# Nine of sixteen contraction steps with seven products, and one sum of weight blocks made by an accumulating DMA

## The chip, the cores and the metric

The kernel runs on one core of a Trainium2 chip. The metric is device time in microseconds (us) of one execution; a profiled execution gives the trace that the views below are taken from. TensorE (PE) does the matrix products, VectorE (DVE) and ScalarE (ACT) the elementwise work, GpSimd (POOL) and SyncE (SP) mostly issue DMAs.

## The reference

The input x has 256 rows (tokens) of 4096 float32 values. Only the attention layer is run (DEPTH is 1), then a final norm:

```python
h = x
h = h + attn_branch(rms_norm(h, norm_attn), w_in_attn, w_out_attn)
return rms_norm(h, final_norm)

def attn_branch(xn, w_in, w_out):
    proj = xn @ w_in                       # 256 x 4096 by 4096 x 16384
    q, k, v, g = jnp.split(proj, 4, axis=-1)
    ...                                    # 32 heads of 128, strictly causal stick-breaking attention
    return (o * jax.nn.silu(g)) @ w_out    # 256 x 4096 by 4096 x 4096
```

Almost all of the work is in the two projections. Their weights are 335 MB, which are read once.

## The kernel before

**Products.** Every float32 operand is split into a high part (cast to fp32r, `wh`, on ScalarE, line 176) and the residual (`wl`, VectorE, function `minus`, line 102). One block product is three matmuls (`mm3`, lines 406 to 408): high by high, low by high, high by low. A block product is a 128x128 block of the rows' side (stationary) by a 128x512 block of weights (moving), summed in one of seven PSUM banks.

**Units and steps.** The projection with w_in is 16 units; each takes a set of 1024 columns, as two groups of 512. The projection with w_out is three units of 1024 columns and two single ones of 512. A unit walks the contraction in 16 steps of 256. A step has a 2x2 of row blocks (two halves of the tokens, two chunks of 128 of the contraction) and a 2x2 of weight blocks (two chunks, two column groups): B11, B21, B12, B22. The plain way takes eight block products. By Strassen and Winograd's scheme seven are enough, but then sums of blocks are needed on both sides. Units 0 and 1 and the first w_out unit are "plain"; 14 w_in units and 2 w_out units are "mixed": the steps in `SEVEN` (2, 4, 6, 8, 10, 12, 13) take seven products and the other nine take eight, in a form that shares the seven banks.

**Weights.** `load(q)` (line 155, SyncE's queue) brings a step's four blocks into one tile `raw` of 128 x 4 x 512 with four DMAs of 256 KB; three such tiles are in turn. `split(n)` makes `wh` and `wl` of one part of a step. A part is a pair of blocks (1024 columns wide) or a single one. In a seven-product step the blocks are used up as they are, B11 and B21's pair first, then B22 alone; then VectorE makes the sums in `raw` itself, a broadcast add of 1024 columns (L165) and two adds of 512 (L168, L169), and the sums are split as two more pairs. Tiles for split pairs are five (`PAIRS`), for singles one (`SINGLES`).

**Order.** The program walks the parts; before a part's products it emits `split` for the parts ahead until more than `PAIRS` pairs or `SINGLES` singles are in the window. Work beside the products (attention of the unit before, reading out the banks, loads) is put at a step of a unit by `at(u, s, ...)` and emitted after that step's products: transposes of the heads at steps 2 and 7, scores one step later, weights of the values and outputs at steps 5, 6, 10 and 11, `heads_parts` at 11 with three spills to DRAM on GpSimd's queue, `combine_early` at 14, `combine_late` at 15 (L352 to L355), the gate and the split of v (L375 to L386) at step 0 of the next unit. A scheduler then reorders instructions within each engine's queue. In the last w_in unit and behind it the spilled parts come back on GpSimd's queue (L485, L489).

**The end.** For the last `KEPT` (= `PAIRS`) parts the products of the second half of the tokens are kept until the first half has been read out, so that its norm and its stores lie beside them (`evac_out` with L537 and L538, `finish` with L554 to L570).

Of the kernel before, what the change touches and what calls it, by code (L numbers as in the profile page):

```python
# [9 lines left out]
F32 = mybir.dt.float32  # L10
# [3 lines left out]
ALU = mybir.AluOpType  # L14
# [4 lines left out]
P = 128  # L19
S = 256  # L20
# [4 lines left out]
CW = 256  # L25
# [15 lines left out]
SEVEN = (2, 4, 6, 8, 10, 12, 13)  # L41
SEVEN_OUT = SEVEN
RAW_BUFS = 3
PAIRS = 5
SINGLES = 1
# [7 lines left out]
EIGHT_FORMS = PLAIN_FORMS + ("S3", "S5")  # L53
SEVEN_FORMS = ("A11", "A12", "A22", "S2", "S3", "S4", "S1")
# [20 lines left out]
def kernel(  # L75
# [41 lines left out]
    for u, (kind, w, cols) in enumerate(units):  # L117
        for s in range(NS):
            if kind == "single":
                if s % 2 == 0:  # L120
                    quads.append(((w, cols[0], s), (w, cols[0], s + 1)))
                b = ((1, 6), (7, 2))[u - LAST + 1]
                which = [plain_part(slice(2 * (s % 2), 2 * (s % 2) + 2), *b)]
            else:
                quads.append(tuple((w, c, s) for c in cols))
                if kind == "plain":
                    which = [
                        plain_part(slice(0, 2), PLAIN["C11"], PLAIN["C21"]),
                        plain_part(slice(2, 4), PLAIN["C12"], PLAIN["C22"]),
                    ]  # L130
                else:
                    which = SEVEN_PARTS if s in (SEVEN if w is w_in else SEVEN_OUT) else EIGHT_PARTS
            for i, (place, prods) in enumerate(which):
                parts.append(
                    dict(u=u, s=s, i=i, last=i == len(which) - 1, place=place, prods=prods, quad=len(quads) - 1,
                         seven=which is SEVEN_PARTS, size=len(range(*place.indices(2 * KT))))
                )
# [7 lines left out]
    raw, wh, wl = {}, {}, {}  # L145

    def load(q):
        if q >= len(quads):
            return
        raw[q] = wp.tile([P, 2 * KT, W], F32, tag="raw", name=f"raw{q}", bufs=RAW_BUFS)  # L150
        for k, (w, blocks, s) in enumerate(quads[q]):
            for chunks in ([slice(0, 1), slice(1, 2)] if q == 0 else [slice(0, 2)]):
                to = slice(KT * k + chunks.start, KT * k + chunks.stop)
                for i, c in enumerate(blocks):
                    nc.sync.dma_start(raw[q][:, to, i * CW : (i + 1) * CW], w[c, s][:, chunks, :])  # L155

    def split(n):
# [4 lines left out]
        r = raw[q]  # L162
        if p["seven"] and p["i"] == 2:

            nc.vector.tensor_tensor(  # L165
                out=r[:, 0:3:2, :], in0=r[:, 0:4:3, :], in1=r[:, 2:3, :].broadcast_to([P, 2, W]), op=ALU.add
            )
            nc.vector.tensor_tensor(out=r[:, 3, :], in0=r[:, 0, :], in1=r[:, 3, :], op=ALU.add)  # L168
            nc.vector.tensor_tensor(out=r[:, 1, :], in0=r[:, 3, :], in1=r[:, 1, :], op=ALU.add)  # L169
# [4 lines left out]
        for c in ([slice(k, k + 1) for k in range(KT)] if n == 0 else [slice(0, size)]):  # L174
            f = r[:, place, :][:, c, :]
            nc.scalar.copy(wh[n][:, c, :], f)  # L176
            minus(wl[n][:, c, :], f, wh[n][:, c, :])
# [7 lines left out]
    def load_x(i):  # L185
        if i >= NS:
            return
        xs[i] = ap.tile([P, KT, S], F32, tag=("one", "two", "vh", "vl")[i % 4], name=f"xs{i}")
# [32 lines left out]
    def build(i, y, seven, what):  # L221
# [17 lines left out]
        tt(out=y[:, 3, :], in0=y[:, 1, :], in1=y[:, 3, :], op=ALU.subtract)  # L239
        tt(out=y[:, 1, :], in0=y[:, 0, :], in1=y[:, 1, :], op=ALU.subtract)  # L240
        tt(out=y[:, 0, :], in0=y[:, 3, :], in1=y[:, 0, :], op=ALU.subtract)
        tt(out=y[:, 2, :], in0=y[:, 2, :], in1=y[:, 0, :], op=ALU.add)
# [20 lines left out]
    load(0)  # L263
    load_x(1)
    load(1)
    load_x(2)
# [82 lines left out]
    def combine_late(bank, one, two):  # L349
# [3 lines left out]
        for t in (1, 0):  # L353
            tt(out=two[:, t, :], in0=bank[5], in1=two[:, t, :], op=ALU.subtract)
# [5 lines left out]
    def new_heads(u):  # L360

        st["qk", u] = ap.tile([P, NT, W], F32, tag="one", name=f"qk_sb{u}")
        st["gv", u] = ap.tile([P, NT, W], F32, tag="two", name=f"gv_sb{u}")
# [140 lines left out]
    def new_h(c):  # L504

        for t in range(NT):
            pool, tag = {NJ - 2: (wp, "s" + "hl"[t]), NJ - 1: (sp, "x" + "hl"[t] + "0")}.get(c, (ep, f"h{c}_{t}"))
            hs[c, t] = pool.tile([P, W], F32, tag=tag, name=f"h{c}_{t}")
# [142 lines left out]
    def products(n, rows=("A11", "A12", "A21", "A22", "S1", "S2", "S3", "S4", "S5")):  # L651
# [19 lines left out]
    for n, p in enumerate(parts):  # L671
# [10 lines left out]
        products(n, ("A11", "A12") if n >= n_parts - KEPT else PLAIN_FORMS + SEVEN_FORMS + ("S5",))  # L682
# [49 lines left out]
```

## Time and profile before

| | |
|---|---|
| median of three runs | 1792.67 us (1787.96 to 1793.42) |
| profiled execution | 1787.47 us, span 1785.8 us |
| mean granted TensorE clock | 0.996 |
| TensorE matmul, busy | 1765.1 us, 8059 instructions |
| VectorE, busy | 1539.7 us, 1885 instructions |
| ScalarE, busy | 1122.8 us, 1533 instructions |
| moved by DMA | 388.81 MB, mean 218 GB/s |

The span runs from the first to the last instruction; the profiled execution's own time is 1.7 us longer. In a view by line, a row has the line, the engine, the operation, out<-in with shapes and the count, then busy us and the mean ns of one, then the idle time before them and what ended it. In a timeline a row has the start, the duration, engine, line and operation, and in brackets the idle time before it. In a table of windows each engine has its busy us and instruction count in a stretch of the span, then the TensorE clock, the share of the DMA engines' time and GB/s.

### The profile page before, as it was taken

How to read it: one execution, taken by the hardware profiler on the slowest of the kernel's cores; microseconds unless marked ns; L12 is line 12 of the kernel's file. 1: busy time of each engine (PE TensorE's matmuls, PEld its weight loads, DVE VectorE, ACT ScalarE, POOL GpSimd, SP SyncE). 2: the span in 40 equal slices, each digit the busy share in tenths (PEclk: the TensorE clock that was granted, in tenths of full speed). 3: DMA queues.
4: the chain of work that ended last, by engine and by line, in shares of the span. 5: the costliest groups of instructions: out<-in, count | busy, mean ns of one | idle time of the engine just before them, and what ended most of it. 6: DMA issues, size and time to landing. Idle time of an engine off the chain costs nothing.

```text
span 1785.8 us, 23623 instructions
## 1 busy us (share of the span) xinstructions
PE 1765.1 (99%) x8059; PEld 1456.9 (82%) x8059; DVE 1539.7 (86%) x1885; ACT 1122.8 (63%) x1533; POOL 68.5 (4%) x135
## 2 busy tenths in 40 slices
PE   9999999999999999999999999999999999999997
PEld 7887888888888888888888888888888878888886
DVE  6678999989898989899999999989989888999863
ACT  6665666666666666666666666666666666665543
POOL 0001000000000000000000000000002201000000
PEclk9999999999999999999999999999999999999998
DMA  9966666566666666666666666757578978778874
GB/s 314 339 196 217 197 187 212 183 212 186 209 195 200 205 198 205 198 207 196 210 194 212 193 209 189 221 174 229 170 223 266 308 231 248 228 225 264 258 239 157
DMA packets 373993, 388.81 MB, mean 218 GB/s; under 512 B 23856, under 2 KB 351792, under 8 KB 373872
## 3 DMA queue, kind: packets, MB, share of 16 engines
q1 hardware_dynamic: 357296, 352.15, 62.7%
q0 software_dynamic: 14992, 32.78, 5.8%
q10 hardware_dynamic: 1584, 2.38, 0.4%
q8 instruction: 63, 1.03, 0.2%
q14 instruction: 58, 0.48, 0.1%
HBM read 370.43 MB, written 16.78 MB: 217 GB/s over the span
## 4 chain that ended last, share of the span: by engine, by line
PE 81%; issue 7%; DVE 4%; DMA 4%; ACT 3%; SPq 1%; POOL 0%; ACTq 0%; POOLq 0%; DVEq 0%
PE acc L406 26%; PE acc L407 26%; PE acc L408 25%; DVE wl L102 2%; ACT wh L176 2%; DMA xr<-in_x_dram 1%; DMA raw<-in_w_in_dram 1%; SPq L155 1%; PE tr L395 1%; DMA raw<-in_w_out_dram 1%; DMA xn<-in_xT_dram 0%; DVE raw L165 0%; DMA xres<-in_x_dram 0%; PE o L407 0%; PE o L408 0%
## 5 line engine op out<-in xcount | busy, mean ns | idle before, releaser
L102 DVE TENSOR_TENSOR wl<-raw,wh 128x1024 fp32r<-128x1024 f32 (+1 forms) x865 | 973.9, 1150 | 190.1 <-ACT wh L176 182.8
L176 ACT CAST wh<-raw 128x1024 fp32r<-128x1024 f32 (+1 forms) x865 | 833.5, 992 | 440.1 <-DVE raw L165 127.5
L406 PE MATMUL acc<-wh,nh 128*128 128x512 f32 x1694 | 669.0, 395 | 0.9 <-DVE qk_sb L352 0.6
L407 PE MATMUL acc<-wl,nh 128*128 128x512 f32 x1694 | 660.5, 390 | 0.0
L408 PE MATMUL acc<-wh,nl 128*128 128x512 f32 x1694 | 660.3, 390 | 0.0
L408 PEld LDWEIGHTS acc<-wh,nl 128*128 128x128 f32 x1694 | 318.0, 188 | 67.4
L407 PEld LDWEIGHTS acc<-wl,nh 128*128 128x128 f32 x1694 | 318.6, 188 | 63.7 <-DVE wl L102 2.8
L406 PEld LDWEIGHTS acc<-wh,nh 128*128 128x128 f32 x1694 | 318.1, 188 | 63.8 <-ACT wh L176 1.0
L165 DVE TENSOR_TENSOR raw<-raw 128x1024 f32<-128x1024 f32 x112 | 136.4, 1218 | 0.1
L407 PE MATMUL acc<-wl,ph 128*128 128x512 f32 x314 | 122.5, 390 | 0.4 <-DVE wl L102 0.2
L408 PE MATMUL acc<-wh,pl 128*128 128x512 f32 x314 | 122.2, 389 | 0.0
L406 PE MATMUL acc<-wh,ph 128*128 128x512 f32 x314 | 122.2, 389 | 0.0
L406 PE MATMUL acc<-wh,sh 128*128 128x512 f32 x256 | 100.3, 392 | 0.6 <-DVE sh L213 0.6
L408 PE MATMUL acc<-wh,sl 128*128 128x512 f32 x256 | 99.7, 390 | 0.6 <-DVE sl L216 0.6
L407 PE MATMUL acc<-wl,sh 128*128 128x512 f32 x256 | 99.9, 390 | 0.3 <-DVE wl L102 0.3
L168 DVE TENSOR_TENSOR raw<-raw 128x512 f32<-128x512 f32 x112 | 77.2, 689 | 2.7
L169 DVE TENSOR_TENSOR raw<-raw 128x512 f32<-128x512 f32 x112 | 76.9, 687 | 1.8
L407 PEld LDWEIGHTS acc<-wl,ph 128*128 128x128 f32 x314 | 58.9, 188 | 13.7 <-DVE wl L102 1.7
L406 PEld LDWEIGHTS acc<-wh,ph 128*128 128x128 f32 x314 | 58.9, 188 | 12.4
L408 PEld LDWEIGHTS acc<-wh,pl 128*128 128x128 f32 x314 | 58.9, 188 | 12.1
L406 PEld LDWEIGHTS acc<-wh,sh 128*128 128x128 f32 x256 | 48.1, 188 | 11.0 <-issue 1.4
L408 PEld LDWEIGHTS acc<-wh,sl 128*128 128x128 f32 x256 | 48.0, 188 | 11.1 <-DVE sl L216 1.1
(158 smaller groups left out, 1436.0 us busy)
## 6 DMA issues: line engine op xcount, KB each, us to landing
raw<-in_w_in_dram SPq DMA_DIRECT2D x1020, 256.0 KB, 4.5
raw<-in_w_out_dram SPq DMA_DIRECT2D x256, 256.0 KB, 4.4
xr<-in_x_dram SPq DMA_DIRECT2D x16, 256.0 KB, 4.8
xn<-in_xT_dram POOLq DMA_DIRECT2D x16, 256.0 KB, 3.9
spill_f<-gated POOLq DMA_DIRECT2D x16, 256.0 KB, 3.8
spill_h<-oh POOLq DMA_DIRECT2D x16, 256.0 KB, 3.2
spill_l<-ol POOLq DMA_DIRECT2D x16, 256.0 KB, 2.5
oh<-spill_h POOLq DMA_DIRECT2D x16, 256.0 KB, 4.9
```

The costliest lines, as they stand in the source:

```text
L102: nc.vector.tensor_tensor(out=out_, in0=full, in1=part.bitcast(F32), op=ALU.subtract)
L155: nc.sync.dma_start(raw[q][:, to, i * CW : (i + 1) * CW], w[c, s][:, chunks, :])
L165: nc.vector.tensor_tensor(out=r[:, 0:3:2, :], in0=r[:, 0:4:3, :], in1=r[:, 2:3, :].broadcast_to([P, 2, W]), op=ALU.add)
L168: nc.vector.tensor_tensor(out=r[:, 3, :], in0=r[:, 0, :], in1=r[:, 3, :], op=ALU.add)
L169: nc.vector.tensor_tensor(out=r[:, 1, :], in0=r[:, 3, :], in1=r[:, 1, :], op=ALU.add)
L176: nc.scalar.copy(wh[n][:, c, :], f)
L395: nc.tensor.transpose(tr[:, k, t * P : (t + 1) * P], st["qk", u][:, t, c : c + P], ident)
L406: nc.tensor.matmul(out_, ah, bh, start=start, stop=False, **kw)
L407: nc.tensor.matmul(out_, ah, bl, start=False, stop=False, **kw)
L408: nc.tensor.matmul(out_, al, bh, start=False, stop=stop, **kw)
```

## The change

Nine steps of a mixed unit take seven products: 1, 2, 4, 5, 7, 9, 10, 12 and 13. Of a step's four blocks only three are in `raw`; B12 goes into a tile `one` of its own, four in turn. In a seven-product step GpSimd then issues a DMA that adds B22 from DRAM onto it, so that `one` holds B12 + B22 when it lands. VectorE makes the other sums: it subtracts `one` from B11 in place (one instruction of 512), and adds that onto B21 and B22 (one broadcast add of 1024). The seven sums differ in sign from the old ones, so the sums on the rows' side (`build`) and one sign in `combine_late` change with them. A seven-product step now has two pairs and three singles instead of three pairs and one single; an eight-product step has its second pair in two tiles, so that it is split with two casts and two residuals of 512. There are four buffers for pairs (and so four kept parts at the end) and three for singles. SyncE issues six DMAs per step, of 256 KB (two) and 128 KB (four).

```diff
-SEVEN = (2, 4, 6, 8, 10, 12, 13)
+SEVEN = (1, 2, 4, 5, 7, 9, 10, 12, 13)
 RAW_BUFS = 3
-PAIRS = 5
-SINGLES = 1
+SUM_BUFS = 4
+PAIRS = 4
+SINGLES = 3
 KEPT = PAIRS
...
 SEVEN_PARTS = (
-    (slice(0, 2), ((1, "A11", 0), (2, "A12", 1))),
-    (slice(3, 4), ((3, "S4", 0),)),
-    (slice(0, 3, 2), ((5, "S1", 0), (7, "S3", 1))),
-    (slice(1, 4, 2), ((4, "A22", 0), (6, "S2", 1))),
+    ((0, 1), ((1, "A11", 0), (2, "A12", 1))),
+    ((2,), ((3, "S4", 0),)),
+    ((3,), ((7, "S3", 0),)),
+    ((0,), ((6, "S2", 0),)),
+    ((1, 2), ((4, "A22", 0), (5, "S1", 1))),
 )
 EIGHT_PARTS = (
-    (slice(0, 2), ((2, "A11", 0), (2, "A12", 1), (4, "A21", 0), (4, "A22", 1))),
-    (slice(2, 4), ((5, "A21", 0), (5, "A22", 1), (3, "S3", 0), (3, "S5", 1))),
+    ((0, 1), ((2, "A11", 0), (2, "A12", 1), (4, "A21", 0), (4, "A22", 1))),
+    ((3, 2), ((5, "A21", 0), (5, "A22", 1), (3, "D1", 0), (3, "D2", 1))),
 )
...
-        raw[q] = wp.tile([P, 2 * KT, W], F32, tag="raw", name=f"raw{q}", bufs=RAW_BUFS)
+        raw[q] = wp.tile([P, 3, W], F32, tag="raw", name=f"raw{q}", bufs=RAW_BUFS)
         for k, (w, blocks, s) in enumerate(quads[q]):
-            for chunks in ([slice(0, 1), slice(1, 2)] if q == 0 else [slice(0, 2)]):
-                to = slice(KT * k + chunks.start, KT * k + chunks.stop)
+            for chunks in ([slice(0, 1), slice(1, 2)] if q == 0 else [slice(0, 2)]) if k == 0 else [slice(1, 2)]:
+                to = slice(k + chunks.start, k + chunks.stop)
                 for i, c in enumerate(blocks):
                     nc.sync.dma_start(raw[q][:, to, i * CW : (i + 1) * CW], w[c, s][:, chunks, :])
+
+    def load_one(q):
+        if q >= len(quads):
+            return
+        one[q] = wp.tile([P, W], F32, tag="one", name=f"one{q}", bufs=SUM_BUFS)
+        w, blocks, s = quads[q][1]
+        for i, c in enumerate(blocks):
+            nc.sync.dma_start(one[q][:, i * CW : (i + 1) * CW], w[c, s][:, 0, :])
+        if q in sums:
+            for i, c in enumerate(blocks):
+                nc.gpsimd.dma_start(one[q][:, i * CW : (i + 1) * CW], w[c, s][:, 1, :], accum_op=ALU.add)
 
     def split(n):
         p = parts[n]
         q = p["quad"]
         if p["i"] == 0 and (n == 0 or parts[n - 1]["quad"] != q):
             load(q + RAW_BUFS - 1)
-        r = raw[q]
+            load_one(q + SUM_BUFS - 1)
+        r, o = raw[q], one[q]
+
         if p["seven"] and p["i"] == 2:
-
+            nc.vector.tensor_tensor(out=r[:, 0, :], in0=r[:, 0, :], in1=o, op=ALU.subtract)
+        if p["seven"] and p["i"] == 3:
             nc.vector.tensor_tensor(
-                out=r[:, 0:3:2, :], in0=r[:, 0:4:3, :], in1=r[:, 2:3, :].broadcast_to([P, 2, W]), op=ALU.add
+                out=r[:, 1:3, :], in0=r[:, 1:3, :], in1=r[:, 0:1, :].broadcast_to([P, 2, W]), op=ALU.add
             )
-            nc.vector.tensor_tensor(out=r[:, 3, :], in0=r[:, 0, :], in1=r[:, 3, :], op=ALU.add)
-            nc.vector.tensor_tensor(out=r[:, 1, :], in0=r[:, 3, :], in1=r[:, 1, :], op=ALU.add)
...
-        for c in ([slice(k, k + 1) for k in range(KT)] if n == 0 else [slice(0, size)]):
-            f = r[:, place, :][:, c, :]
+        if n == 0 or 3 in place:
+            pieces = [(slice(k, k + 1), at_) for k, at_ in enumerate(place)]
+        else:
+            pieces = [(slice(0, size), place[0])]
+        for c, at_ in pieces:
+            f = o.rearrange("p (a c) -> p a c", a=1) if at_ == 3 else r[:, at_ : at_ + c.stop - c.start, :]
             nc.scalar.copy(wh[n][:, c, :], f)
             minus(wl[n][:, c, :], f, wh[n][:, c, :])
...
         for t in (1, 0):
-            tt(out=two[:, t, :], in0=bank[5], in1=two[:, t, :], op=ALU.subtract)
+            tt(out=two[:, t, :], in0=bank[5], in1=two[:, t, :], op=ALU.add)
```

More of the change, by code (lines that the diff above doesn't have):

```diff
@@ L135 @@
                     dict(u=u, s=s, i=i, last=i == len(which) - 1, place=place, prods=prods, quad=len(quads) - 1,
-                         seven=which is SEVEN_PARTS, size=len(range(*place.indices(2 * KT))))
+                         seven=which is SEVEN_PARTS, size=len(place))
                 )
@@ L142 @@
             ends[p["u"], b] = (n, k)
-    raw, wh, wl = {}, {}, {}
+    raw, one, wh, wl = {}, {}, {}, {}
+    sums = {p["quad"] for p in parts if p["seven"]}
     def load(q):
@@ L187, in load_x @@
             return
-        xs[i] = ap.tile([P, KT, S], F32, tag=("one", "two", "vh", "vl")[i % 4], name=f"xs{i}")
+        xs[i] = ap.tile([P, KT, S], F32, tag=("qk", "gv", "vh", "vl")[i % 4], name=f"xs{i}")
         if i:
@@ L648, with products @@
     at(LAST, 4, new_h, NJ - 1)
[L651 removed]
+    def products(n, rows):
         p = parts[n]
```

33 lines of the change are left out of this document (19 added, 14 removed).

## The prediction

> **What bounds the kernel now.** I read the busy shares and the chain first.
>
> ```profile
> span 1785.8 us, 23623 instructions
> PE 1765.1 (99%) x8059; PEld 1456.9 (82%) x8059; DVE 1539.7 (86%) x1885; ACT 1122.8 (63%) x1533; POOL 68.5 (4%) x135
> ...
> PE 81%; issue 7%; DVE 4%; DMA 4%; ACT 3%; SPq 1%; POOL 0%; ACTq 0%; POOLq 0%; DVEq 0%
> ```
>
> The matmuls carry the chain and VectorE is second. A busy matmul row overlaps its neighbour, so the price of one matmul is read from starts in the timeline:
>
> ```profile
> 1080.87 0.39 PE L406 MATMUL acc<-wh,nh 128*128 128x512 f32 x1
> 1081.09 0.39 PE L407 MATMUL acc<-wl,nh 128*128 128x512 f32 x1
> 1081.32 0.39 PE L408 MATMUL acc<-wh,nl 128*128 128x512 f32 x1
> 1081.55 0.39 PE L406 MATMUL acc<-wh,nh 128*128 128x512 f32 x1
> ```
>
> Three matmuls, one product, take 1081.55 - 1080.87 = 0.68 us, 0.227 us each. I take an eight-product step as 24 x 0.2267 = 5.44 us, a seven-product step as 4.76 us. Next the windows of one steady unit (heads of the unit before beside the projection) and of the last w_in unit:
>
> ```profile
> core 0: us, PE busy (x) PEld busy (x) DVE busy (x) ACT busy (x) POOL busy (x), PEclk, DMA share, GB/s
> 1000.00:1088.05 88.05, 88.05 (x412) 73.03 (x409) 79.83 (x93) 57.00 (x75) 1.61 (x3) 1.00 0.64 200
> 1340.70:1428.80 88.10, 87.77 (x407) 72.42 (x405) 77.73 (x90) 56.40 (x74) 19.12 (x36) 1.00 0.92 288
> ```
>
> A unit is 88.05 us, TensorE never idles in it, its clock is full, and VectorE has 88.05 - 79.83 = 8.2 us left. So TensorE sets the end in every middle unit, with VectorE close behind.
>
> **Term 1: products removed.** Two more steps of each mixed unit drop one product: 2 x 3 = 6 matmuls. There are 14 mixed w_in and 2 mixed w_out units, so 96 matmuls go (the compiled orders have 7344 and 7248 into the accumulators). 96 x 0.2267 = 21.8 us off the path; a w_in unit could shrink by 1.36 us to 86.7 us. The Trainium skill (TensorE: Matmul & The Clock Gate, Part 1) gives 215.7 ns from start to start for 512 columns at full clock; by that the term would be 20.7 us. The trace's 0.227 us decides.
>
> **Term 2: VectorE and ScalarE.** Durations by form, from the groups by line:
>
> ```profile
> L102 DVE TENSOR_TENSOR wl<-raw,wh 128x1024 fp32r<-128x1024 f32 x751 | 900.4, 1221 | 182.9 <-ACT wh L176 175.8 <-DMA raw<-in_w_out_dram 2.0
> L176 ACT CAST wh<-raw 128x1024 fp32r<-128x1024 f32 x751 | 771.1, 1049 | 411.0 <-DVE raw L165 127.5 <-DVE raw L169 116.7 <-PE acc L408 68.9
> ...
> L165 DVE TENSOR_TENSOR raw<-raw 128x1024 f32<-128x1024 f32 x112 | 136.4, 1218 | 0.1
> ...
> L102 DVE TENSOR_TENSOR wl<-raw,wh 128x512 fp32r<-128x512 f32 x114 | 77.9, 683 | 7.2 <-ACT wh L176 7.0
> L168 DVE TENSOR_TENSOR raw<-raw 128x512 f32<-128x512 f32 x112 | 77.2, 689 | 2.7
> L169 DVE TENSOR_TENSOR raw<-raw 128x512 f32<-128x512 f32 x112 | 76.9, 687 | 1.8
> L176 ACT CAST wh<-raw 128x512 fp32r<-128x512 f32 x114 | 70.2, 616 | 29.1 <-DMA raw<-in_w_in_dram 25.4 <-DMA raw<-in_w_out_dram 3.6
> ```
>
> Back to back, VectorE instructions overlap a little too:
>
> ```profile
> 1074.36 0.68 DVE L355 TENSOR_TENSOR gv_sb<-acc,gv_sb 128x512 f32<-128x512 f32 x1
> 1074.96 1.21 DVE L102 TENSOR_TENSOR wl<-raw,wh 128x1024 fp32r<-128x1024 f32 x1
> 1076.09 0.68 DVE L102 TENSOR_TENSOR vl<-gv_sb,vh 128x512 fp32r<-128x512 f32 x1
> ```
>
> So from start to start a 512 costs 0.60 us and a 1024 costs 1.13 us.
> - Seven-product step before: four 1024 (three residuals, L165) and three 512 (one residual, L168, L169): 4 x 1.13 + 3 x 0.60 = 6.32 us. After: three 1024 (two residuals, the broadcast add) and four 512 (three residuals, the subtract): 5.79 us.
> - Eight-product step before: 2 x 1.13 = 2.26 us; after, its second pair lies in two tiles and is split in two: 1.13 + 2 x 0.60 = 2.33 us.
> - Unit before: 7 x 6.32 + 9 x 2.26 = 64.6 us; after: 9 x 5.79 + 7 x 2.33 = 68.4 us: 3.8 us more. By the mean durations instead (6.94 and 2.44 against 6.40 and 2.59) it is 75.7 - 70.6 = 5.1 us. I take 3.8, since VectorE's queue is nearly always full, and keep 5.1.
>
> VectorE then needs 79.83 + 3.8 = 83.6 of 86.7 us, 3.1 us spare instead of 8.2; with 5.1 it is 1.8. The same sum for ScalarE's casts: 7 x 3.76 + 9 x 2.10 = 45.2 before, 9 x 3.95 + 7 x 2.28 = 51.5 after, 57.0 + 6.3 = 63.3 us: not the bound.
>
> Average room is not enough; the split-ahead window also shrinks. A pair tile now waits for the fourth pair before it and a single for the third single before it. So in two adjacent seven-product steps the second step's first single cannot be cast before TensorE has left the first step's first single, six products (4.1 us) ahead of its own use; the step's last pair comes 3 products later. In the compiled order I followed VectorE and ScalarE by hand from there, with 0.60/1.13 us, 1.05 and 0.62 us casts, and the attention work where the order puts it:
> - Steps 9 and 10: the scores' vector work lies in step 10's split. The last residual is done about 0.15 us after TensorE wants it.
> - Steps 4, 5 and 12, 13: just in time, 0 to 0.3 us spare.
> - Steps 1 and 2: the bank combination and the gate of the last unit lie between. The gate's ScalarE work enters here:
>
> ```profile
> 1075.07 0.62 ACT L386 CAST vh<-gv_sb 128x512 fp32r<-128x512 f32 x1 [0.91 <-DVE gv_sb L355]
> 1075.60 0.63 ACT L375 ACTIVATE gl<-gv_sb 128x512 f32<-128x512 f32 x1
> 1076.26 0.63 ACT L376 ACTIVATE gl<-gl 128x512 f32<-128x512 f32 x1
> 1076.92 0.63 ACT L377 ACTIVATE gl<-gl 128x512 f32<-128x512 f32 x1
> ```
>
> Counted from TensorE's start of step 15, the last combination (L355) is done at 11.2 us; the cast and three activations hold ScalarE 0.62 + 3 x 0.65 = 2.6 us, to 13.9; then VectorE has left the gate's two 512, two single residuals, the 1024 add, one more single and the last pair: 5 x 0.60 + 2 x 1.13 = 5.3 us, plus 0.6 us in which the last cast waits for the add. That ends at 19.8 to 19.9; TensorE wants it at 19.3. A stall of 0.6 us. At the border itself bank 5 is read out at about 9.4 us and wanted at 9.5, because the compiled order moves step 1's first products ahead of bank 5's: no stall, nothing spare.
>
> So 0.75 us per w_in unit, 14 x 0.75 = 10.5 us. Bounds: 0 (each place errs by 0.3 us either way) and the second rival's.
>
> **Term 3: the transfers.** SyncE issues six instead of four per step, and GpSimd two accumulating ones in each seven-product step:
>
> ```profile
> L155 SPq DMA_DIRECT2D raw<-in_w_in_dram x1028: 327/610/1890, 0.8 to 1404.5; - x172
> ...
> DMA to landing us min/median/max: 2.5/4.5/8.4
> ```
> ```profile
> L480 POOL DMA_DIRECT2D spill_f<-gated x16: 544/544/549, 173.3 to 1502.3; - x16
> ```
>
> SyncE: 6 x 0.61 = 3.7 us in a step of 4.76: hidden. GpSimd: 2 x 0.54 us: hidden; behind the accumulates in its queue stand the spills and their loads, all used at least one step later. The accumulate itself is not in the trace. Nearest are plain loads that GpSimd issues (L485, the parts read back from the spill):
>
> ```profile
> DMA to landing us min/median/max: 3.0/5.1/7.3
> ```
>
> The tightest one is step 1's. Its buffer comes free in step 13, by my walk 12.9 us before ScalarE casts the sum. Of that go 2 x 0.61 issue, 4.5 plain landing, 2 x 0.54 issue: 6.1 us are left for the accumulate. At 3.0 or 5.1 us it is hidden, at 7.3 us 1.2 us late. I take 5.1, as half the bytes of those loads but with the destination read too. The Trainium skill (DMA: Bandwidth & Descriptors, Anatomy of one DMA) fits 2.0 us + bytes / 436 GB/s: 2.3 us for 128 KB, an estimate from that page; by it the sum is the same.
>
> Extra bytes: 9 x 0.25 = 2.25 MB per unit. The last w_in unit moved 288 x 88.1 = 25.4 MB with 0.92 x 88.1 = 81 us of DMA time, 3.2 us per MB; 7.2 us more (14.4 if the destination's read counts alike) make 88 to 95 of 86.7 us. Part of its traffic is read back for the next unit and can slide: I take 1 us, bounds 0 and 9. Other units go from 0.64 x 88.05 = 56 to 64 or 71 us: hidden.
>
> **Term 4: the tail.** Four instead of five parts keep their second-half products for the end, 4 x 6 x 0.227 = 5.4 us of cover instead of 6.8:
>
> ```profile
> 1767.71 0.75 DVE L537 TENSOR_TENSOR h<-acc,xres 128x256 f32<-128x256 f32 x2 [4.49 <-PE acc L408]
> ...
> 1773.10 1.60 ACTq L570 DMA_DIRECT2D out_dram<-h  x2
> 1774.51 0.76 DVE L537 TENSOR_TENSOR h<-acc,xres 128x256 f32<-128x256 f32 x2 [2.27 <-PE acc L408]
> 1774.96 0.39 ACT L538 ACTIVATE sq<-h 128x256 f32<-128x256 f32 x1 [1.28 <-DVE h L537]
> ```
>
> ScalarE finishes the first half at 1773.10 + 1.60 = 1774.70, 0.26 us before it must square the second. With 1.36 us less cover it is 1.1 us late: +1 us. Signs, form names and tile tags cost nothing.
>
> **Sum.** -21.8 + 10.5 + 1 + 1 = -9.3 us. Against the profiled execution (1787.47 us) that is 1778.2; the median shown is 1792.67, 0.3% above it, and the forecast is given against the median: 1783.4 us. About 0.3% (5.4 us) is what a measurement of this kernel tells from no change.
>
> **Rivals.**
> 1. All stalls are hidden. For it: TensorE had no idle time in the steady unit and the compiler moved products to the tight places. -21.8 + 1 to 2: 1772.
> 2. VectorE becomes the pace (slower). In each seven-product step the last cast waits for the add (1.22 + 1.05 us) while VectorE has one 512 residual to do (1.13 + 0.60 us): 0.55 us idle. In my walk other work fills about half of these. If none does, 9 x 0.55 = 5.0 us, and buffers that are full add 0.5: 83.6 + 5.5 = 89.1 us a unit, 14 x 1.05 = +15, less 2 x 1.36 in the w_out units, plus 1: +13, 1806. It decides from 88.05 - 83.6 = 4.4 us of idle VectorE per unit. For it: the row of waits for ScalarE (182.9 us), a shallower window. Against: the old order's sum-then-cast waits (L165, L169) are gone, since the accumulated tile is cast without VectorE.
> 3. The accumulate lands late. At 8 us the first seven-product step of 15 units gets its sum 1.9 us late with ScalarE and VectorE queued behind it: +28, so 1811. It decides from 6.1 us, and it makes the kernel slower from about 6.8.
> 4. The last w_in unit and the w_out units run out of DMA: +8 on the forecast, 1791.
>
> **Numbers.** Forecast with stalls of 0.3 to 1.1 us a unit: 0.42; rival 1: 0.18; rival 2: 0.20; rival 3: 0.12; rival 4: 0.08. Faster: 0.18 and nearly all of 0.42, 0.58; same: rival 4 and the edges of the forecast and of rival 2, 0.14; slower: 0.28. The range runs from 1770 (rival 1, no tail cost) to 1807 (rival 2); it leaves out rival 3 and the worst of rival 2. The forecast's own range is 1776 to 1789.
>
> **What would show it.** Right: a steady unit of about 87.4 us with VectorE busy near 83.6 us, TensorE waits for wl in step 2 of a unit, GpSimd's accumulate landing under 6 us, the first half's finish reaching into the second's square. Wrong: a unit at 86.7 us (rival 1); above 88 us with VectorE idle over 4.4 us (rival 2); casts of the tile "one" that wait for DMA (rival 3); a long unit only at 1340 us and after (rival 4).

## The result, and the profile after

The changed kernel takes 1817.44 us (median of four runs, 1816.43 to 1821.46) and the kernel before, on the same chip, 1790.78 us (1787.96 to 1793.42). The ratio is 1.0155, 95% interval 1.0136 to 1.0174: 26.7 us slower, above the range's end of 1807. The page of the profiled execution after, busy shares and chain:

```profile
span 1814.7 us, 26374 instructions
PE 1769.4 (98%) x7963; PEld 1436.1 (79%) x7963; DVE 1595.4 (88%) x2237; ACT 1198.5 (66%) x1921; POOL 324.8 (18%) x427
...
PE 59%; DVE 13%; DMA 10%; issue 8%; ACT 5%; SPq 4%; POOL 0%; ACTq 0%; DVEq 0%; POOLq 0%
```

The 96 matmuls are gone (8059 to 7963 rows), yet the span is 28.9 us longer than before. TensorE's share of the chain falls from 81 to 59%; VectorE (4 to 13%) and DMA (4 to 10%) take its place. A steady stretch, from the table of windows:

```profile
core 0: us, PE busy (x) PEld busy (x) DVE busy (x) ACT busy (x) POOL busy (x), PEclk, DMA share, GB/s
1000.00:1090.00 90.00, 89.28 (x407) 72.30 (x406) 83.52 (x110) 61.20 (x95) 17.43 (x21) 1.00 0.80 223
```

VectorE has 6.5 us of 90 idle, the clock is full, and the DMA share is 0.80 where it was 0.64. The unit's length is read from the timeline, from the first transpose of the heads of one unit to that of the next. So each span falls into four stretches:

| us | to the first transposes | unit 1 | 14 mixed units, mean of one | the rest | span |
|---|---|---|---|---|---|
| before | 111.3 | 96.6 | 88.36 | 340.8 | 1785.8 |
| after | 111.9 | 100.7 | 89.23 | 352.8 | 1814.7 |
| after without the accumulating transfers (1) | 111.8 | 100.7 | 88.28 | 347.2 | 1795.6 |
| the same with the old seven steps (8) | 112.4 | 93.7 | 87.98 | 341.1 | 1779.0 |

The loss of 28.9 us: 0.6 + 4.1 + 14 x 0.87 + 12.0. The matmuls alone should have given -19 us in the 14 units and -2.7 us in the rest.

What holds TensorE in the middle units is best read at its weight loads, which run ahead of the matmuls and so show short waits that the matmul rows hide. The waits of that queue from 300 to 1360 us (twelve units), as "engine tile line <- what it waited for: us in total, times, longest", after:

```profile
PEld acc L431 <- DVE wl L106: 13.4, 36, 0.5
PEld o L430 <- ACT gated L489: 11.5, 24, 0.7
PEld acc L430 <- DVE gv_sb L378: 9.1, 11, 0.9
PEld acc L430 <- DVE qk_sb L376: 7.1, 8, 2.0
```

and before:

```profile
PEld o L406 <- ACT gated L465: 4.8, 24, 0.2
PEld acc L407 <- DVE wl L102: 2.4, 12, 0.2
PEld acc L406 <- ACT wh L176: 1.0, 1, 1.0
```

Three kinds of waits have grown, each by half a us to 1.4 us a unit: residuals that come late (`wl`), the copy of the gate that the heads' outputs wait for (`gated`), and at the unit's border the read-out of the banks (`gv_sb`, `qk_sb`).

### The profile page after: what moved, and what is told of

It is laid out like the page before. It is cut to its first block, busy times and chain, and to the rows that moved or that the text cites. A ratio compares the mean times of both kernels' runs of the same rounds, so it can differ in the third digit from the quotient of the medians.

```text
span 1814.7 us, 26374 instructions
## 1 busy us (share of the span) xinstructions
PE 1769.4 (98%) x7963; PEld 1436.1 (79%) x7963; DVE 1595.4 (88%) x2237; ACT 1198.5 (66%) x1921; POOL 324.8 (18%) x427
## 4 chain that ended last, share of the span: by engine, by line
PE 59%; DVE 13%; DMA 10%; issue 8%; ACT 5%; SPq 4%; POOL 0%; ACTq 0%; DVEq 0%; POOLq 0%
PE acc L431 19%; PE acc L432 18%; PE acc L430 18%; DVE wl L106 7%; DMA raw<-in_w_in_dram 5%; SPq L160 4%; ACT wh L197 3%; DVE raw L184 2%; DMA one<-in_w_in_dram 1%; DMA raw<-in_w_out_dram 1%; DMA one<-in_w_out_dram 1%; DVE raw L182 1%; PE o L430 1%; DMA xn<-in_xT_dram 1%; PE tr L419 1%
## 5 line engine op out<-in xcount | busy, mean ns | idle before, releaser
L197 ACT CAST wh<-raw 128x1024 fp32r<-128x1024 f32 (+1 forms) x929 | 748.6, 833 | 391.5 <-DVE raw L184 150.8
L106 DVE TENSOR_TENSOR wl<-raw,wh 128x1024 fp32r<-128x1024 f32 (+1 forms) x929 | 863.2, 951 | 113.3 <-ACT wh L197 112.3
L430 PE MATMUL acc<-wh,nh 128*128 128x512 f32 x1666 | 656.8, 396 | 8.8 <-DVE gv_sb L378 4.9
L432 PE MATMUL acc<-wh,nl 128*128 128x512 f32 x1666 | 647.9, 390 | 0.0
L430 PEld LDWEIGHTS acc<-wh,nh 128*128 128x128 f32 x1666 | 312.9, 188 | 80.7 <-DVE gv_sb L378 10.5
L171 POOL DMA_DIRECT2D one<-in_w_in_dram x252 | 221.1, 1072 | 728.8 <-DMA one<-in_w_in_dram 313.8
L106 DVE TENSOR_TENSOR wl<-one,wh 128x512 fp32r<-128x512 f32 x320 | 218.9, 684 | 17.8 <-ACT wh L197 15.0
L197 ACT CAST wh<-one 128x512 fp32r<-128x512 f32 x320 | 197.6, 617 | 46.7 <-PE acc L432 39.2
L184 DVE TENSOR_TENSOR raw<-raw 128x1024 f32<-128x1024 f32 x144 | 175.3, 1217 | 0.5
L430 PE MATMUL acc<-wh,ph 128*128 128x512 f32 x294 | 115.2, 393 | 5.0 <-ACT h L645 3.0
L182 DVE TENSOR_TENSOR raw<-raw,one 128x512 f32<-128x512 f32 x144 | 98.7, 686 | 2.3 <-DMA one<-in_w_out_dram 0.7
L432 PEld LDWEIGHTS acc<-wh,pl 128*128 128x128 f32 x294 | 55.5, 189 | 11.3
```

What stands on the lines that cost most here:

```text
L106: nc.vector.tensor_tensor(out=out_, in0=full, in1=part.bitcast(F32), op=ALU.subtract)
L171: nc.gpsimd.dma_start(one[q][:, i * CW : (i + 1) * CW], w[c, s][:, 1, :], accum_op=ALU.add)
L182: nc.vector.tensor_tensor(out=r[:, 0, :], in0=r[:, 0, :], in1=o, op=ALU.subtract)
L184: nc.vector.tensor_tensor(out=r[:, 1:3, :], in0=r[:, 1:3, :], in1=r[:, 0:1, :].broadcast_to([P, 2, W]), op=ALU.add)
L430: nc.tensor.matmul(out_, ah, bh, start=start, stop=False, **kw)
L432: nc.tensor.matmul(out_, al, bh, start=False, stop=stop, **kw)
```

## The experiments

My theory after the result: the accumulating transfers cost most of it, by landing late or by delaying the raw loads. The rival: VectorE's work, or where it lies, and not the transfers. The times below stand against the kernel before on the same chip, whose medians were 1789 to 1791 us. TensorE, VectorE and ScalarE take their instructions in the same order in kernels 1, 5 and the changed one; likewise in 3, 8 and 11, in 13 and 16, and in 2 and 6. The other edits move some of them, because the build sorts each queue by its own plan.

**1. Without the accumulating transfers**

```diff
-        if q in sums:
-            for i, c in enumerate(blocks):
-                nc.gpsimd.dma_start(one[q][...], w[c, s][:, 1, :], accum_op=ALU.add)
```

> The changed kernel without the accumulating DMAs (the tile then holds one block and not the sum of two; all else is issued as before). If VectorE's load sets the pace (83.6 us of work in a unit that TensorE could do in 86.7), nothing is gained: 1810 to 1820 us. If the accumulates' traffic or their landing holds the casts up, the kernel falls to 1775 to 1795 us.

1797.11 us, ratio 1.0036 (1.0023 to 1.0048). The transfers cost 20.3 us of 1817.4. Its weight loads' waits, same stretch:

```profile
PEld acc L428 <- DVE wl L106: 13.8, 37, 0.5
PEld o L427 <- ACT gated L486: 11.6, 24, 0.7
PEld acc L427 <- DVE gv_sb L375: 4.3, 12, 0.9
PEld acc L427 <- DVE qk_sb L373: 0.9, 2, 0.5
```

Only the border changes: bank read-outs from 16.2 to 5.2 us, which is 0.9 us a unit. The residuals and the gate stay, so these are not the transfers' doing. And with no cost of transfers at all, nine steps are still 6 us over the kernel before.

**2. Without VectorE's subtraction** (`raw` minus `one`, L182, left out)

> The changed kernel without VectorE's subtract of 512 columns in the nine seven-product steps: 9 x 0.60 = 5.4 us less VectorE work per unit, nothing else taken away. If VectorE sets the pace, the 1.6 to 2.5 us a unit that are lost come back: 1775 to 1790 us. If the transfers do, at most a third of it: 1805 to 1817 us.

1826.70 us (1821.80 to 1831.85), 1.0201 (1.0167 to 1.0235): 9 us over the changed kernel, with less work for VectorE. Its waits in that stretch are 19.1 us for `wh` and 10.6 for `gv_sb`. Less work for VectorE did not help here; but the build also moved its instructions, so this run neither prices the subtraction nor rules VectorE's work out.

**3. The old seven steps in the new structure** (`SEVEN = (2, 4, 6, 8, 10, 12, 13)`)

> The changed kernel with the seven steps of before (2, 4, 6, 8, 10, 12, 13) in place of nine: the same products as before, but sums, tiles, buffers and DMAs as after. VectorE's work per unit is 7 x 5.79 + 9 x 2.33 = 61.5 us against 64.6 before. If VectorE's load in nine steps is the cause, 1787 to 1795 us (as before the change). If the smaller window, the split loads or the accumulates cost by themselves, 1800 to 1820 us.

1833.65 us, 1.0237 (1.0183 to 1.0291). A miss for both theories: fewer transfers, and slower. The timelines of ScalarE, VectorE and TensorE at a border show the late landing of the sum as the prediction's third rival had it:

```profile
1105.06 1.14 ACT L197 CAST wh<-one 128x512 fp32r<-128x512 f32 x2 [4.89 <-DMA one<-in_w_in_dram]
1106.23 0.69 DVE L106 TENSOR_TENSOR wl<-one,wh 128x512 fp32r<-128x512 f32 x1 [4.45 <-ACT wh L197]
1106.84 0.68 DVE L379 TENSOR_TENSOR gv_sb<-acc,gv_sb 128x512 f32<-128x512 f32 x1
1107.57 0.79 PE L430 MATMUL acc<-wh,nh 128*128 128x512 f32 x1 [2.59 <-DVE gv_sb L379]
1108.16 0.63 PE L431 MATMUL acc<-wl,nh 128*128 128x512 f32 x1
1108.59 0.63 PE L432 MATMUL acc<-wh,nl 128*128 128x512 f32 x1
```

ScalarE waits 4.89 us for the tile, VectorE behind it, the bank's read-out stands next in VectorE's queue, and TensorE waits for the bank. Then its matmuls start 0.43 us apart instead of 0.23: the granted clock is at half. This happens twelve times in the kernel, 44 us at half clock in all, which by itself can cost up to 22 us (an estimate: half of that time).

**4. The old sums and buffers with nine steps** (the kernel before with the new `SEVEN`)

> The kernel before, with its three sums on VectorE and its buffers, but with the nine steps of the change. VectorE's work grows by 2 x (6.32 - 2.26) = 8.1 us to 88 us per unit, more than TensorE's 86.7. If VectorE sets the pace this is slower than the change: 1820 to 1850 us. If the accumulate, the smaller window or the loads are to blame, it is faster than the change: 1775 to 1810 us.

1887.30 us, 1.0540 (1.0521 to 1.0560). VectorE is busy 1670.2 us here and takes 40% of the chain. So here VectorE's work does hold the kernel. The new sums do relieve it; without them nine steps would cost 97 us.

**5. The same transfer, not adding**

```diff
-                nc.gpsimd.dma_start(one[q][...], w[c, s][:, 1, :], accum_op=ALU.add)
+                nc.gpsimd.dma_start(one[q][...], w[c, s][:, 1, :])
```

> Leaves the addition out of the second transfer: the same bytes go from the same GpSimd queue into the same tile, after the same plain load, but are written over it and not added (so the sum of two blocks is only its second block). If it is the addition itself that costs (its landing and its issue), this comes near the kernel without the second transfer: 1797 to 1802 us, unit 88.2 to 88.5. If it is the extra traffic and the two transfers in a row, it stays with the changed kernel: 1812 to 1820 us, unit 89.0 to 89.3.

1805.49 us, 1.0084 (1.0069 to 1.0099), between both: a second transfer of the same bytes into the same tile costs 8.4 us, the adding another 12. Issue on GpSimd fell from 221.1 to 135.1 us for 252 transfers and landing from 5.2 to 3.7 us.

**6. Neither transfers nor subtraction** (1 and 2 together)

> Leaves out both the accumulating transfers and VectorE's subtraction ahead of the third part, so two of the four sums are not formed. It asks what the remaining 27 us are. If VectorE's load paces the kernel once the accumulating transfers are gone (84.1 us busy of a 88.2 us unit), taking nine subtractions from it brings the unit to about 86.6 and the time to 1797 - 14 x 1.6 = 1775 us. If VectorE has enough room, the time stays at 1795 to 1799 us; what is left is then in the waits that are outside the 14 mixed units and in the loop of the raw tiles.

1807.30 us, 1.0091 (1.0076 to 1.0106): 10 us slower than 1 with 87 us less for VectorE (1508.3 against 1595.5). The border's `gv_sb` waits went from 4.3 to 13.9 us. As in 2, the build's order moved. Against 2, whose order it shares, it gives the price of the transfers a second time: about 19 us (the runs of 2 differ by 10 us among themselves).

**7. Six tiles for the sum, two for single blocks**

```diff
-SUM_BUFS = 4
+SUM_BUFS = 6
-SINGLES = 3
+SINGLES = 2
```

> Six tiles for the accumulated sum instead of four, so that each plain load and accumulating transfer starts two steps (about 11 us) earlier; the room comes from the single split blocks, two buffers instead of three. If the late landing of the sum is what costs, most of the 20 us comes back: 1797 to 1805 us, unit 88.2 to 88.7. If the extra traffic costs by delaying the raw blocks, it stays at 1812 to 1822 us, whatever the number of tiles. The lost single buffer can cost 0 to 5 us in both.

1859.45 us, 1.0394 (1.0374 to 1.0413). The cost of the lost single tile drowned what was asked: weight loads wait 39.3 us for `wh` and 19.5 for `wl` in twelve units. It says nothing on the transfers. The two edits together cost 2.4 us a unit (91.64 against 89.23), most likely for the third single tile; the order of many instructions moved too.

**8. Seven steps, no accumulating transfers** (1 and 3 together)

> The old seven steps in the changed kernel's structure, with the accumulating transfers left out (so one sum is not formed). If the new buffers and the new order of the sums cost nothing by themselves, this is at the time of the kernel before or a little under it: 1785 to 1793 us, unit 87.8 to 88.0, because its TensorE work is the same and its VectorE work is less. If the new structure costs (four instead of five pairs of split blocks, five parts to a step), it is at 1797 or above.

1781.43 us, 0.9952 (0.9937 to 0.9967). TensorE's weight loads have one row of waits left, in the twelve units:

```profile
PEld o L427 <- ACT gated L486: 4.8, 24, 0.2
```

So with seven steps the buffers, parts and signs cost nothing on balance. Against kernel 1, two more steps cost: 7.0 us in unit 1, 4 us in the 14 units where their products give back 19, and 6.1 us in the rest where they give 2.7. Against 3, with the same order, it says that even seven steps lose 52 us to the transfers.

**9 and 10. The plain load ahead of the raw loads**, with nine and with seven steps

```diff
-            load_one(q + SUM_BUFS - 1)
...
+        if 3 in place:
+            load_one(q + SUM_BUFS)
```

> Nine steps as in the changed kernel, with all transfers kept; only the place of the plain load changes. It is issued right after the part that last reads the tile that it refills, ahead of the next step's four raw loads in SyncE's queue and not behind them; with the four issues of 0.58 us and the two to three products in between it should start 3 to 6 us earlier, and the accumulating transfer behind it too. If the late landing of the sum is what the accumulating transfer costs, most of its 20 us comes back: 1798 to 1808 us, unit 88.2 to 88.8. If it is the extra traffic on the DMA engines, which stays the same, 1813 to 1820 us.

> The same early plain load with the old seven steps; it stands against the seven-step run at 1833.7 us and the one without the accumulating transfers at 1781.4 us. In the former the cast of the summed tile waited 4.9 us for its landing in one border between units, and TensorE 2.6 us for the bank behind it. If that late landing is the cause, starting 3 to 6 us earlier takes the wait at the border away: 1782 to 1795 us, unit 87.9 to 88.5. If the traffic is the cause, 1825 to 1835 us.

With seven steps 1800.10 us, 1.0051 (1.0036 to 1.0066): 33.6 of the 52 us come back, and nothing waits for the accumulated tile any more. With nine 1825.75 us, 1.0193 (1.0178 to 1.0208): nothing comes back. Late landing of the sum is most of the loss with seven steps, and not the cause with nine; the changed kernel's own list of who waited for its accumulating DMAs says the same (operation, then durations in ns as min/median/max; then us and times):

```profile
L171 POOL DMA_DIRECT2D one<-in_w_in_dram x252: 851/891/1822, 177.0 to 1412.4; - x126
...
who waited for it (us, times):
  ACT wh L197: 2.3, 2
  DVE raw L182: 0.7, 2
...
DMA to landing us min/median/max: 3.0/5.3/8.2
```

3.0 us in the whole run. What is late at its borders are the raw loads. The timelines of SyncE's queue, GpSimd, ScalarE, VectorE and TensorE there, after:

```profile
1073.87 5.12 SPq L160 DMA_DIRECT2D raw<-in_w_in_dram  x8
1074.42 1.79 POOL L171 DMA_DIRECT2D one<-in_w_in_dram  x2 [3.84 <-DMA one<-in_w_in_dram]
1079.37 1.05 ACT L197 CAST wh<-raw 128x1024 fp32r<-128x1024 f32 x1 [2.33 <-DMA raw<-in_w_in_dram]
1080.46 1.23 DVE L106 TENSOR_TENSOR wl<-raw,wh 128x1024 fp32r<-128x1024 f32 x1 [1.34 <-ACT wh L197]
1087.37 0.68 DVE L376 TENSOR_TENSOR qk_sb<-acc,qk_sb 128x512 f32<-128x512 f32 x1
1088.10 0.50 PE L430 MATMUL acc<-wh,nh 128*128 128x512 f32 x1 [0.50 <-DVE qk_sb L376]
```

and at the same place in kernel 1:

```profile
1066.85 6.28 SPq L160 DMA_DIRECT2D raw<-in_w_in_dram  x8
1071.06 1.06 ACT L194 CAST wh<-raw 128x1024 fp32r<-128x1024 f32 x1 [1.04 <-PE acc L429]
```

From the first raw issue to the cast it is 4.2 us without the transfers, where the data are there in time, and 5.5 us with a pair of accumulating transfers in flight. Over the run the raw loads (256 KB) land in 4.2 us instead of 3.7.

The pair goes out at this place in every unit from the second to the fourteenth: 60.9 to 63.8 us after the unit's first transposes, beside the eight raw loads, which are issued from 61.1 to 67.2. By the landing times in the trace, the length of the unit follows the last of the eight: 88.1 to 88.6 us where it lands by 70.6, 88.9 to 89.5 where it lands at 71.2 to 71.8, and 90.1 and 90.6 where it lands at 72.3. In the median it lands at 70.0 us in kernel 1, 70.5 in kernel 5 and 71.3 in the changed kernel, and their mixed units take 88.28, 88.74 and 89.23 us. In kernel 9 ScalarE waits 1.0 to 3.1 us for raw loads in each of these units; the earlier plain load did not help what was late.

**11. The sum on GpSimd, seven steps**

```diff
+        if p["seven"] and p["i"] == 0:
+            nc.gpsimd.tensor_tensor(out=o, in0=o, in1=r[:, 2, :], op=ALU.add)
```

in place of the transfers.

> Seven steps; the accumulating transfers are replaced by an addition on GpSimd from the raw block that is loaded anyway, into the same tile, so every sum is formed, with no extra bytes and no second transfer. If only the transfer and its landing cost, and GpSimd adds 128x512 in about 1 us beside the other engines, this is at the time without accumulating transfers, 1781 to 1787 us, and below the kernel before. If GpSimd's addition is slow or lengthens VectorE's instructions while it runs, casts wait for it as they waited for the transfer: 1795 to 1830 us.

1788.15 us (ten runs), 0.9982 (0.9973 to 0.9992): the only kernel with all its sums that is below the one before, by 0.18%, less than the prediction's bound for no change. The groups by line, GpSimd's addition and VectorE's residual of a pair:

```profile
L179 POOL TENSOR_TENSOR one<-one,raw 128x512 f32<-128x512 f32 x112 | 189.1, 1688 | 1024.6 <-DMA raw<-in_w_in_dram 750.8 <-DVE wl L106 87.3 <-DVE raw L183 59.9
L106 DVE TENSOR_TENSOR wl<-raw,wh 128x1024 fp32r<-128x1024 f32 x431 | 562.2, 1320 | 98.0 <-ACT wh L196 92.0 <-DMA raw<-in_w_in_dram 3.5 <-DMA raw<-in_w_out_dram 0.8
```

The same residual in kernel 8, without GpSimd's addition:

```profile
L106 DVE TENSOR_TENSOR wl<-raw,wh 128x1024 fp32r<-128x1024 f32 x431 | 521.4, 1223 | 126.1 <-ACT wh L194 120.6 <-DMA raw<-in_w_in_dram 4.2
```

**12, 13 and 16. The transfers into tiles apart**: 13 has no transfers and three tiles for the plain loads; 12 adds the transfers into two tiles that nothing reads, 16 the same, held back to the plain load's landing by a two-element copy into the tile that is added to (in 12 the copy went into a third tile and held nothing back). The edit of 16:

```diff
-SUM_BUFS = 4
+SUM_BUFS = 3
...
+            for t in apart:
+                nc.gpsimd.tensor_copy(out=t[:, 0:2], in_=one[q][:, CW - 1 : CW + 1])
             for i, c in enumerate(blocks):
-                nc.gpsimd.dma_start(one[q][...], w[c, s][:, 1, :], accum_op=ALU.add)
+                nc.gpsimd.dma_start(apart[i], w[c, s][:, 1, :], accum_op=ALU.add)
```

> Nine steps. The accumulating transfers add into two tiles that nothing reads, at the time at which they ran before (a two-element GpSimd copy waits for the plain load); so one sum of four is not formed, the traffic is the same, and no part of the computation waits for it. Three tiles for the plain loads make the room. If the traffic costs, by making the raw loads land later, this takes about what the changed kernel does: 1810 to 1820 us, raw loads landing in 4.2 to 4.5 us, ScalarE waiting over 30 us for raw loads. If what waits for the sum costs, it is at the time without these transfers: 1795 to 1800 us.

> The control to the run with the sum apart: no accumulating transfers, three tiles instead of four for the plain loads. Without a second transfer behind it the plain load has time enough in three tiles: 1795 to 1800 us, as with four. If it takes more, the fewer tiles cost that much in the run with the sum apart too.

> Nine steps; the accumulating transfers add into two tiles that nothing reads, but a two-element GpSimd copy from the plain load's tile into each ahead of its transfer now holds them back until the plain load has landed. So one sum of four is not formed, the traffic runs all the way, and no part of the computation waits for it. If the traffic costs: 1808 to 1820 us, mixed units about 88.9 to 89.2 us. If the waiting for the sum costs: 1796 to 1802 us, mixed units 88.0 to 88.4 us, as without the transfers.

13: 1796.51 us, 1.0033 (1.0021 to 1.0045), so three tiles cost nothing where no transfer follows. 12: 2062.69 us, 1.1515 (1.1478 to 1.1553), and no answer: with nothing tied to them the build put all 288 transfers into the first 640 us. 16: 1813.24 us, 1.0123 (1.0101 to 1.0144), by its time the verdict "traffic"; but the stretches say otherwise. The first 13 of its 14 mixed units take 1146.0 us against 1145.3 in 13 (1157.6 in the changed kernel), with no more bank waits than kernel 1:

```profile
PEld acc L436 <- DVE wl L106: 13.4, 36, 0.5
PEld o L435 <- ACT gated L494: 11.6, 24, 0.7
PEld acc L435 <- DVE gv_sb L383: 4.6, 12, 0.9
PEld acc L435 <- DVE qk_sb L381: 0.6, 1, 0.6
```

Its loss against 13, which has the same order, is 5.8 us in unit 1, 6.3 in the last mixed unit and 5.3 in the rest. The first two I put down to GpSimd's held-back queue, for the changed kernel does not have them (0.0 and 1.0 us there); that was not tested. The rest is like the changed kernel's 6.7. So this traffic costs 0.7 us in the middle units and some 5 us in the rest. That is not a matter of the DMA engines being fuller there (their share is 0.84 in the middle and 0.82 in the rest): one wait of TensorE for a bank's copy grew from 1.7 us in 13 to 3.1 in 16, with the clock at half behind it.

What differs in the middle units is where the transfers fall. In 16, at a border like those above, the pair goes out 5 us after the eight raw loads, and the cast waits for no load:

```profile
984.48 4.73 SPq L160 DMA_DIRECT2D raw<-in_w_in_dram  x8
988.69 1.06 ACT L203 CAST wh<-raw 128x1024 fp32r<-128x1024 f32 x1 [1.04 <-PE acc L437]
994.06 1.78 POOL L177 DMA_DIRECT2D apart<-in_w_in_dram  x2
```

In its units 2 to 14 no accumulating transfer is issued between 59 and 70.7 us after the first transposes, and the last of the eight loads lands at 69.9 in the median, as without transfers.

**14 and 15. Eight steps in four and in two neighbouring pairs**, no accumulating transfers: `SEVEN = (1, 2, 4, 5, 9, 10, 12, 13)` and `(1, 2, 4, 6, 8, 10, 12, 13)`

> Eight steps of seven products, (1, 2, 4, 5, 9, 10, 12, 13), in four pairs of neighbours, without the accumulating transfers (one sum not formed). It stands against the next run, which has the same work in two pairs. If neighbouring steps make the stalls, this keeps most of those of the nine-step kernel: unit about 88.4 us (87.98 - 0.68 + 1.1), 1795 to 1800 us. If VectorE's whole load makes them, both runs are equal, between seven steps (1781 us) and nine (1797 us): 1783 to 1792 us.

> Eight steps, (1, 2, 4, 6, 8, 10, 12, 13), in two pairs of neighbours; the rest as in the run with four pairs. If neighbouring steps make the stalls, half of them go: unit about 87.7 us, 1783 to 1788 us, at least 7 us under the run with four pairs. If VectorE's whole load makes them, the same as the run with four pairs within 3 us.

14: 1839.06 us, 1.0277 (1.0249 to 1.0306). 15: 1802.97 us, 1.0070 (1.0045 to 1.0095). VectorE's work is the same within 2.3 us, so its amount is refuted as the cause of the 36 us between them. But neighbouring steps as such are not the cause either: kernel 1 has those four pairs and a ninth step, and is 42 us faster than 14. In 14 the wait for the gate has taken over:

```profile
PEld o L427 <- ACT gated L486: 29.2, 23, 3.0
```

So it is likely that the loss depends on which of the heads' work falls into which step's splits; no run shows that by itself.

**17. The sum on VectorE, seven steps**: the line of 11 with `nc.vector`, ahead of the subtraction

> Seven steps in the new structure, with the sum added on VectorE from the raw block, right ahead of the subtraction that reads it; every sum is formed. It puts 112 x 0.60 = 67 us back on VectorE, 4.2 us a unit. If VectorE's whole load decides, its 1492 + 77 = 1569 us is as much as with GpSimd's addition (1570, where it is slowed) and the time is 1785 to 1790 us. If the place in VectorE's queue decides, the addition delays the bank read-outs at the border between units as the waits for the sum did: 1790 to 1800 us.

1820.07 us, 1.0151 (1.0128 to 1.0175): 32 us slower than on GpSimd with VectorE busy 1547.5 instead of 1570.5 us, waits for the gate 15.7 us. Of the 32 us, 13 lie in the last mixed unit alone (102.0 against 88.8). Above both expectations, on the side of the place in the queue.

**18. The changed kernel with three tiles for the sum**

> The changed kernel with three tiles for the sum instead of four, and the real accumulating transfers. If the tie to the sum makes the loss, the sum has one step less to land and the time is above the changed kernel: 1820 to 1850 us, middle units 89.2 us or more, with casts that wait for the summed tile. If the phase of the transfers between the raw loads makes it, the middle units come down to those of the paced run, 88.1 to 88.4 us, and the time to 1800 to 1812 us.

1914.05 us, 1.0703 (1.0679 to 1.0727). Who waited for the accumulating DMAs:

```profile
who waited for it (us, times):
  ACT wh L197: 136.1, 32
  DVE raw L182: 25.8, 13
```

With the traffic of 16 and one tile less than the changed kernel the sum is late at nearly every border, and the middle units take 95.5 us. Four tiles are just enough for the sum to be in time, three are not.

## Why the prediction was wrong

The forecast was -9.3 us and the result +26.7. In spans, from kernel to kernel: the new structure with the old seven steps gave -6.8 us (before to 8), for which the forecast had no term; two more steps gave +16.6 (8 to 1), where terms 1 and 2 had -11.3; the transfers gave +19.1 (1 to the changed kernel), where term 3 had +1.

**Term 1 (-21.8 us)** went as counted in matmul rows. Back to back they still start 0.227 us apart (1086.76, 1086.99, 1087.22 us at a border after). The waits took more than it gave.

**Term 2, the stalls: one of the two steps that failed, by its size and by two kinds of waits that it left out.** Taken: 0.75 us a unit, all of it `wl`: 0.6 in steps 1 and 2, 0.15 in 9 and 10. Measured without the transfers (kernel 1 against 8, twelve units): `wl` 13.8 us or 1.15 a unit (by counting products, 0.30 us at the end of step 2, 0.46 at the end of step 10 and 0.36 at the end of step 13, so in pairs that the walk had looked at, but with other sizes); the gate's copy 11.6 against 4.8 us, 0.57 a unit, which the walk did not follow at all; the border 5.2 us, 0.43 a unit, where I wrote "no stall, nothing spare". Together 2.15 us of waits at the weight loads for the 0.75; some of it is absorbed, and the unit itself lost 1.66 us (its 1.36 us of products and 0.30 more), over 14 units 23 us for the 10.5. VectorE's 83.6 us were nearly right: 83.52 of 90 us, which is 82.8 of an 89.2 us unit.

**Rival 2** gave the unit almost to the tenth, 89.1 us against 89.23, and its sign was there too (a unit above 88 us, VectorE idle for 6.5 us of 90, over the 4.4 named). That is luck: without the transfers, which are no part of this rival, the unit is 88.28. Nor do the runs bear out its reason, a VectorE with too much to do: kernels 6, 14 and 15 have less work for VectorE than kernel 1, and 17 less than 11, and all four are slower. So within these kernels the amount does not decide (in kernel 4, with 1670.2 us, it may). The order of the queues moved in all four and is the likeliest cause; no run moved the order alone.

**Term 3, the transfers: the other step that failed, by "hidden".** They cost 20.3 us (kernel 1). Their own landing, 5.2 to 5.3 us for the 5.1 taken, was right, and the wait for the sum is only 3.0 us. What I left out is what they do to the others: 13.3 us in the middle units, where the pair goes out among the raw loads of the border and these land late, and 5.6 us in the rest. GpSimd's issue, taken at 0.54 us from the spills, took 0.89 us in the median. Rival 3's mechanism is real, but in kernels 3 and 18, not in this one. Rival 4 saw the last units at 8 us; the rest lost 12.0, but 6.1 of it is there without transfers (1 against 8).

**Unit 1: a missing term.** Unit 1 is 7.0 us longer with nine steps than with seven (kernel 1 against 8; with transfers, after against 3, 6.6), and the forecast had nothing for it. More steps with seven forms mean more sums and splits of the row blocks there: VectorE is busy 86.7 us in unit 1 of kernel 1 and 82.9 in that of kernel 8. But that is not what decides: kernels 14 and 15 have eight such steps each and VectorE is busy 86.4 and 86.3 us, yet the unit takes 101.5 us in 14 and 95.3 in 15. What differs is the wait for the gate's copy, 5.4 us in the matmul rows of 14 and 1.5 in 15 (4.3 in kernel 1, 0.2 in 8). Part of the loss is TensorE's clock, here in the timeline of TensorE and the windows around it, after:

```profile
171.57 0.58 PE L430 MATMUL o<-ah,vh 128*128 128x256 f32 x1 [3.14 <-ACT gated L489]
...
173.44 0.63 PE L431 MATMUL acc<-wl,sh 128*128 128x512 f32 x1
173.87 0.63 PE L432 MATMUL acc<-wh,sl 128*128 128x512 f32 x1
```
```profile
170.00:174.00 4.00, 2.43 (x9) 2.24 (x10) 3.96 (x7) 2.96 (x6) 0.54 (x1) 0.65 0.92 268
174.00:178.00 4.00, 4.00 (x11) 3.13 (x10) 2.80 (x7) 1.53 (x2) 2.63 (x5) 0.50 0.55 180
178.00:182.00 4.00, 4.00 (x19) 3.28 (x19) 2.75 (x6) 1.79 (x5) 1.94 (x3) 1.00 1.15 314
```

After a wait of 3.14 us the granted clock is 0.50: 11 matmuls in the 4 us from 174 to 178 instead of 19. The trace's record of the granted clock has it at half for 6.8 us, so this stall cost about 3 us more; the drop in kernel 3 shown above lasted 3.4 us. The Trainium skill (TensorE: Matmul & The Clock Gate, HAM oscillation) says that a gap of TensorE over about 3.4 us drops the clock to half. Here 3.14 us did it, and 2.59 us in kernel 3.

**Term 4 (+1)** is not separated: kernel 8 has the same tail, and its rest is within 0.3 us of the kernel before, so it is at most small.

**What stays open.** The traces of the changed kernel and of 16 agree that the moment of the transfers makes the border late, and not their bytes nor the wait for the sum (3.0 us). But no run moved the moment alone: 16 also cuts the tie to the sum and has one tile less. Nor was a rule found for which steps may take seven products.

## What to carry to other kernels

Before counting on removed matmuls, list what each queue holds in order at the tightest place (here the border between units) and look at TensorE's weight loads: in kernel 1 they show 2.55 us of waits a unit where the matmul rows show 0.33. An extra transfer is not hidden because its own landing is in time; ask which loads it shares the moment with, and what stands behind their consumers. And an edit that takes work away can cost more than it saves when the queue's order moves with it.

## What the runs showed of the hardware

- An accumulating DMA of 128 KB took GpSimd 0.89 us to issue and 5.2 us to land; the same transfer not adding (kernel 5) took 135.1 / 252 = 0.54 us and 3.7 us. In kernel 12, where the accumulating ones run in a row, they landed in 3.6 us.
- GpSimd's 128x512 float32 addition took 1.69 us against VectorE's 0.69, and 112 of them lengthened VectorE by 78 us (1570.5 against 1492.2): 0.70 us each. The Trainium skill (SBUF — State Buffer, SBUF: two separate sides) says that a GpSimd instruction that reads SBUF and a VectorE one with two inputs from SBUF lock each other out. The longer residual (1320 against 1223 ns) agrees.
- The granted clock fell to half after waits of TensorE well under 3 us, but not after all of them: in kernel 3 twelve times, for 3.4 us each (once 6.8), after waits of 1.8 to 3.2 us; in the kernel before not after one of 2.40 us at 169.8 us.
- In kernel 12 from 740 to 1450 us TensorE's matmul rows had 0.8 us of waits and full clock, and its matmuls started 0.233 us apart instead of 0.227 (1063.81 to 1065.21 us for six). No run explains it.
